# A two-layer encoder trunk on one core: head by quarters of the features, uL, silu and casts earlier in the transitions

## The chip, the cores and the metric

One core of a Trainium2 chip runs the whole program in one launch. The metric is the device time of one execution in microseconds. TensorE does the matmuls, VectorE (DVE in the profile), ScalarE (ACT) and GpSimd (POOL) do the rest, and SyncE (SP) issues the transfers from HBM.

## The reference, cut to what matters

Two layers, each an FFN, a token mixer and an FFN; x is 256 tokens by 1024 features, float32.

```python
for layer in range(DEPTH):
    mod = (silu(c) @ w_ada[layer] + b_ada[layer]).reshape(b, N_SUB, 3, 1, D_MODEL)
    u = standardize(x) * (1 + mod[:, 0, 1]) + mod[:, 0, 0]
    g, up = split(u @ w_ffn_in[layer, 0], 2)                  # 1024 x 5632
    f = (silu(g) * up) @ w_ffn_out[layer, 0]                  # 2816 x 1024
    x = layer_norm(ALPHA * x + 0.5 * (1 + mod[:, 0, 2]) * f, ln_g[layer, 0], ln_b[layer, 0])
    u = standardize(x) * (1 + mod[:, 1, 1]) + mod[:, 1, 0]
    m = hybrid_mixer(u, positions, ...)                       # SSD heads and attention heads
    x = layer_norm(ALPHA * x + (1 + mod[:, 1, 2]) * m, ln_g[layer, 1], ln_b[layer, 1])
    ...                                                       # a second FFN, as the first
```

`mod` is one vector of nine chunks of 1024 for each layer: shift, scale and gate for each of three sublayers.

## The kernel before, in words

Tokens lie in two tiles of 128, t = 0 and 1. Every operand of a large product is kept as a high part (a cast to float32r) and a low part (what the cast left over), and a product is three matmuls: high by high, high by low, low by high. For activations the parts are `uH` and `uL`, for weights `h...` and `l...` (`hg` and `lg` of the gate, `hu` and `lu` of the up half, `ho` and `lo` of the output weights, `hqk` and `lqk` of the mixer's first columns). The high part of a weight is a cast on ACT (`hi`, "h" in the orders), the low part a subtraction on VectorE (`step`, "l" or "a"), 128 x 1024 elements each.

Weights stream in one planned list of 512 KB halves. `issue_loads` keeps nine raw buffers filled; a buffer is free when the subtraction, or the sum of a modulation vector, has read it. The modulation rows are summed against silu(c): on VectorE in the stream, and in the head chunk 0 (shift) on TensorE and chunk 1 (scale) on VectorE (`adh_step`).

The **head** is the first FFN's beginning. It runs through the list `HEAD`, by two halves of the 1024 features: statistics of a tile (n), rstd (r), normalise and turn (x), sums (a), copying them (c), making columns of them (p), modulation of the half (m), weight casts (h, l), the high and low products of columns block b, gate or up i (`U`, `L`), silu and multiplication (e, `evac_a`), turning h (t). This order is strict on TensorE, VectorE and ACT: `in_order(True, pe=True)` makes each engine issue in the order of the program.

Behind it come **blocks** of 256 hidden columns. Block b makes `ob` (48 matmuls of 256 columns for each of two halves j), then the output product of block b-1 (`acc`, 512 columns); silu and a multiplication `hf` turn `ob` into h, which `split` gives parts hH and hL. Here the order within an engine is made by a scheduler from priorities, save for ties set by `order` and `keep`.

Between two sublayers `cross` runs a **transition**: the same residual and norm chain for both tiles (c0 and c1: gate, mean, acc, rstd, squares, rstd2, turn, us, u, m0, l0, m1, and l1 at the end), with the rest of the old sublayer's products (d0 to d3), weight casts (h, l) and the first products of the next sublayer for tile 0 (`P` columns, parts, k range; part 0 is uH by high weights, 1 uL by high weights, 2 uH by low weights) between the steps. The strings FFN_TO_MIX, MIX_TO_FFN and FFN_TO_FFN are that order, and it is strict on all three engines. In such a string "0 m0" makes `um` of tile 0's first half on ACT, "0 l0" subtracts uH from it to give uL on VectorE, and "e" (`evac0`) evacuates the first product bank: an ACT copy before a mixer, silu on ACT and hf on VectorE before an FFN. There are two transitions from FFN to mixer, two from mixer to FFN and one from FFN to FFN.

`setup_mixer` makes the mixers' constants (rotary angles, exponentials) and is called in the blocks of the first FFN.

Of the kernel before, what the change touches and what calls it, by code (L numbers as in the profile page):

```python
# [20 lines left out]
P = 128  # L21
# [21 lines left out]
XAT = 2  # L43
# [5 lines left out]
              "1 acc,P01 02 07,l,1 rstd,0 m0,1 squares,P2 0 07,P2 2 03,P3 0 03,0 l0,P01 1 03,P23 1 03,P3 0 47,1 rstd2,0 m1,"  # L49
              "1 turn,0,P01 1 47,1 us,1 u,l,P2 2 47,P23 1 47,l,l,e,P3 2 07,1,h,h,h").split(",")  # L50
MIX_TO_FFN = ("l,d0,h,h,d1,d2,d3,0 mean,h,0 acc,0 rstd,0 squares,l,0 rstd2,h,0 turn,1 gate,1 gate,0 us,0 u,1 mean,"
              "1 acc,P01 02 07,l,1 rstd,0 m0,1 squares,h,P2 0 07,P2 2 03,P3 0 03,0 l0,P01 1 03,P23 1 03,P3 0 47,1 rstd2,0 m1,"
              "1 turn,0,P01 1 47,1 us,1 u,l,P2 2 47,P23 1 47,l,l,e,P3 2 07,1,h").split(",")
FFN_TO_FFN = ("h,l,d0,0 mean,d1,0 acc,0 rstd,h,h,d2,d3,0 squares,l,0 rstd2,h,l,h,h,0 turn,1 gate,1 gate,0 us,0 u,1 mean,"
              "1 acc,P01 02 07,l,1 rstd,0 m0,1 squares,P2 0 07,P2 2 03,P3 0 03,0 l0,P01 1 03,P23 1 03,P2 2 47,P3 0 47,"
              "1 rstd2,0 m1,1 turn,0,P01 1 47,1 us,1 u,l,l,e,P23 1 47,P3 2 07,1,h").split(",")
# [8 lines left out]
HEAD = ("b,n0,r0,a,n1,x0,a,a,a,c0,r1,x1,a,a,a,p0,a,p1,h,m,h,h,l,l,h,l,h,l,U00,a,U01,a,L00,L01,a,a,c0,U10,a,a,U11,"  # L65
        "a,h,a,p0,L10,p1,L11,+,h,m,k,h,h,h,l,l,U00,l,U01,l,h,l,L00,L01,e00,h,U10,e10,l,h,l,U11,t00,h,l,L10,t10,l,"
        "L11,h,l,e01,t01,h,l,e11,h,l,t11").split(",")

@with_exitstack
def kernel(  # L70
# [124 lines left out]
    def issue_loads(upto):  # L195
        while pos["load"] < min(upto, 2 * len(items)):
            n = pos["load"]
            i, h = divmod(n, 2)
            kind, key, src = items[i]
            if kind == "pair":  # L200
                half = src[h].rearrange("(k p) c -> p k c", p=P)
            else:
                half = src.rearrange("(h k p) c -> h p k c", h=2, p=P)[h]
            shape = {"cols": [4, BC], "pair": [4, BC], "adh": [2, 512]}.get(kind, [1, D])
# [15 lines left out]
    ADA = ("ada", "adh")  # L220

    def hi_step():
# [6 lines left out]
        shape = [D] if kind == "rows" else [4, BC]  # L229
# [11 lines left out]
    def step(n=1):  # L241
        for _ in range(n):
# [6 lines left out]
            if kind in ADA:  # L249
                pos["hi"] = max(pos["hi"], k + 1)  # L250
                {"ada": ada_step, "adh": adh_step}[kind](key, raws.pop(k), h)
# [36 lines left out]
    def setup_cond():  # L288
        crow = tp.tile([KT, P], F32, tag="row8", name="crow", bufs=1)
        nc.sync.dma_start(crow, c_in.rearrange("o (k p) -> (o k) p", p=P))  # L290
        nc.sync.dma_start(xs[:, 0, :], x_in[0, 0:P, :])
# [4 lines left out]
        issue_loads(XAT)  # L296
        nc.sync.dma_start(xs[:, 1, :], x_in[0, P:2 * P, :])
# [44 lines left out]
    half_mods = {}  # L342

    def adh_step(key, raw, k):
        ch, h, q = key
        if ch == 1:
            if q == 0 and k == 0:
                half_mods[ch] = wtile([512], f"adv_{h}")
            acc = half_mods[ch]
            for i in range(2):  # L350
                kt = 4 * q + 2 * k + i
                if kt == 0:
                    V.tensor_scalar(acc, raw[:, i, :], cT[:, 0:1], None, op0=ALU.mult)
                else:
                    V.scalar_tensor_tensor(acc, raw[:, i, :], cT[:, kt:kt + 1], acc, op0=ALU.mult, op1=ALU.add)
            return
        if q == 0 and k == 0:
            half_mods[ch] = mps(f"adh{ch}_{h}")
        pa = half_mods[ch]
        for i in range(2):  # L360
            j = 32 * (2 * k + i)
            PE.matmul(pa[j:j + 32, :], lhsT=cw[:, 4 * q + 2 * k + i, :], rhs=raw[:, i, :],
                      start=(q == 0), stop=(q == 1), tile_position=(0, j))

    def adh_copy(h):
        cpy = wtile([512], f"adc_{h}")
        S.copy(cpy, half_mods[0])
        half_mods[0] = cpy

    def adh_post(ch, h):  # L370
        cpy = half_mods.pop(ch)
        if (0, 0) not in mods:
            mods[0, 0] = sm.tile([P, 2, KT], F32, tag="mod", name="mod0_0", bufs=3)
        pp = mps(f"pm_{ch}_{h}")
        for k in range(4):
            PE.matmul(pp[:, k:k + 1], lhsT=cpy[:, k * P:(k + 1) * P], rhs=ones[:, 0:1] if ch else sel1,
                      start=True, stop=True)
        V.scalar_tensor_tensor(mods[0, 0][:, ch, 4 * h:4 * h + 4], pp[:, 0:4], float(ch),
                               bcol[0][:, ch * KT + 4 * h:ch * KT + 4 * h + 4], op0=ALU.add, op1=ALU.add)
# [260 lines left out]
    class Ffn:  # L640
# [41 lines left out]

        def evac(self, o, name):
            sg = tp.tile([P, BC], F32, tag="sg", name="sg" + name)
            S.activation(sg, o[:, 0:BC], AF.Silu)
            hf = tp.tile([P, BC], F32, tag="hf", name="hf" + name)
            V.tensor_tensor(hf, o[:, BC:2 * BC], sg, op=ALU.mult)
            return hf
# [24 lines left out]
        def plan_head(self):  # L713
            for h in range(2):
                for ch in range(2):
                    for q in range(2):
                        plan("adh", (ch, h, q), w_ada[0, q * 512:(q + 1) * 512, ch * D + h * 512:ch * D + (h + 1) * 512])
                r = slice(h * 512, (h + 1) * 512)
                for b in range(NA):
                    plan("pair", f"{b}_{h}", [self.win[r, c + b * BC:c + (b + 1) * BC] for c in (0, DFF)])  # L720

        def head(self):

            norm, pts, ws = {}, {}, {}

            def form(b, i, low):
                if low == 0 and i == 0:
                    ws[b] = take("pair", f"{b}_{half}")
                for t in range(T):
                    if (t, b) not in self.oa:  # L730
                        self.oa[t, b] = gps(f"oa_{t}{b}") if b == 0 else apt(f"oa_{t}{b}")
                    o = self.oa[t, b][:, i * BC:(i + 1) * BC]
                    w = ws[b][i][low]
                    for n, a in enumerate((uH,) if low else (uH, uL)):
                        for k in range(4):
                            PE.matmul(o, lhsT=a[:, t, 4 * half + k, :], rhs=w[:, k, :],
                                      start=(half == 0 and i == 0 and low == 0 and n == 0 and k == 0),
                                      stop=(half == 1 and i == 1 and low == 1 and k == 3))

            half, got = 0, [0, 0]  # L740
            for fn in HEAD:
# [6 lines left out]
                elif op == "x":  # L748
                    for h in range(2):
                        pts[args[0], h] = turn_norm(0, 0, args[0], *norm[args[0]], h, apt(f"pt_{args[0]}_{h}"))  # L750
# [4 lines left out]
                elif op == "s":  # L755
                    setup_mixer()
                elif op == "c":
                    adh_copy(got[0])
                elif op == "p":
                    adh_post(args[0], got[args[0]])  # L760
                    got[args[0]] += 1
                elif op == "m":
                    advance(modulate(0, 0, {(t, half): pts[t, half] for t in range(T)}))
# [636 lines left out]
```

## Time and profile before

| | |
|---|---|
| three runs | 1075.52, 1075.60, 1075.69 us (median 1075.6) |
| profiled execution | 1074.92 us, span 1073.2 us |
| TensorE busy | 1031.1 us, 96% of the span |
| VectorE busy | 825.4 us, 77% |
| ACT busy | 580.9 us, 54% |
| mean rate of the transfers | 239 GB/s |

The profiled execution's time is its span, from the first instruction to the last, and 1.7 us around it. Times in rows are microseconds from the span's start. A window's PEclk is the clock that TensorE was granted: 1.00 is 2.4 GHz and 0.50 is 1.2 GHz. Ends of matmuls are modelled, so starts are the better measure of pace. An idle time in square brackets is the engine's wait before an instruction, with what ended it.

### The profile page before, as it was taken

What the parts mean: (1) busy time and instruction counts of PE and PEld (TensorE: products, weight loads), DVE (VectorE), ACT (ScalarE), POOL (GpSimd) and SP (SyncE); (2) the same over time, 40 slices, a digit from 0 to 9 for tenths busy, and PEclk for the clock granted to TensorE, in tenths of its full rate; (3) what the DMA queues carried; (4) which work ended last, traced back from release to release, by engine and by line L of the source; (5) the groups of instructions that cost most, each with busy time, mean ns of one, the idle gap of its engine ahead of it and who ended that gap; (6) DMA issues with size and microseconds to landing.
All of it is one profiled execution on the core that took longest, in us unless ns stands there. A gap on an engine that the chain in (4) does not pass through costs nothing.

```text
span 1073.2 us, 19053 instructions
## 1 busy us (share of the span) xinstructions
PE 1031.1 (96%) x7433; PEld 944.3 (88%) x7433; DVE 825.4 (77%) x1284; ACT 580.9 (54%) x1046; POOL 36.1 (3%) x79
## 2 busy tenths in 40 slices
PE   4999999989999999999999999999999999999996
PEld 2899999879897899999989999998899879999995
DVE  5788699688998798768588868847899878756454
ACT  3474434378756755343477433536876578535241
POOL 0000000010000100000010000000000010000000
PEclk9999999999999999999999999999999999999998
DMA  9989799948456389879547979883664628866411
GB/s 341 319 298 370 273 306 407 306 138 254 134 188 225 99 304 341 286 294 361 199 138 249 335 296 377 282 280 107 199 209 150 213 91 302 282 221 216 158 41 39
DMA packets 162559, 258.25 MB, mean 241 GB/s; under 512 B 10807, under 2 KB 125983, under 8 KB 162469
## 3 DMA queue, kind: packets, MB, share of 16 engines
q1 hardware_dynamic: 162468, 257.04, 69.6%
q8 instruction: 58, 0.95, 0.4%
q14 instruction: 33, 0.26, 0.1%
HBM read 255.96 MB, written 1.05 MB: 239 GB/s over the span
## 4 chain that ended last, share of the span: by engine, by line
PE 77%; DVE 10%; ACT 7%; issue 3%; DMA 2%; POOL 1%; SPq 0%; DVEq 0%; POOLq 0%; ACTq 0%
PE ob L108 38%; PE acc L108 18%; PE oa L108 5%; PE ocx L108 2%; PE accx L108 2%; PE ovx L108 2%; DVE xs L108 2%; ACT uH L108 2%; ACT um L108 1%; PE oqkx L108 1%; PE ozx L108 1%; ACT junk L108 1%; DVE acc L108 1%; PE pr L108 1%; DVE lg L108 1%
## 5 line engine op out<-in xcount | busy, mean ns | idle before, releaser
L108 PE MATMUL ob<-uH,hg 128*128 128x256 f32 x576 | 162.6, 282 | 0.0
L108 PE MATMUL ob<-uL,hg 128*128 128x256 f32 x576 | 162.2, 282 | 0.0
L108 PE MATMUL ob<-uH,lg 128*128 128x256 f32 x576 | 161.8, 281 | 0.3 <-DVE lg L108 0.3
L108 PE MATMUL ob<-uH,lu 128*128 128x256 f32 x576 | 162.0, 281 | 0.0
L108 PE MATMUL ob<-uH,hu 128*128 128x256 f32 x576 | 161.9, 281 | 0.0
L108 PE MATMUL ob<-uL,hu 128*128 128x256 f32 x576 | 161.7, 281 | 0.0
L108 PE MATMUL acc<-ho,hH 128*128 128x512 f32 x352 | 137.5, 392 | 1.0 <-ACT ho L108 1.0
L108 PE MATMUL acc<-lo,hH 128*128 128x512 f32 x352 | 137.8, 391 | 0.7 <-DVE lo L108 0.7
L108 PE MATMUL acc<-ho,hL 128*128 128x512 f32 x352 | 137.2, 390 | 0.0
L108 ACT ACTIVATE sgb<-ob 128x256 f32<-128x256 f32 x72 | 27.6, 383 | 202.2 <-PE ob L108 201.8
L108 DVE TENSOR_TENSOR lo<-raw_o,ho 128x1024 fp32r<-128x1024 f32 x88 | 105.6, 1220 | 14.4 <-ACT ho L108 7.2
L108 PEld LDWEIGHTS ob<-uH,hg 128*128 128x128 f32 x576 | 108.3, 188 | 6.2 <-issue 2.5
L108 PEld LDWEIGHTS ob<-uH,lu 128*128 128x128 f32 x576 | 110.1, 191 | 1.2 <-issue 1.2
L108 PEld LDWEIGHTS ob<-uH,lg 128*128 128x128 f32 x576 | 110.2, 191 | 0.6 <-DVE lg L108 0.5
L108 PEld LDWEIGHTS ob<-uL,hg 128*128 128x128 f32 x576 | 108.1, 188 | 2.5
L108 DVE TENSOR_TENSOR lg<-raw_g,hg 128x1024 fp32r<-128x1024 f32 x84 | 101.2, 1221 | 11.2 <-ACT hg L108 5.6
L108 PEld LDWEIGHTS ob<-uH,hu 128*128 128x128 f32 x576 | 108.4, 188 | 0.5 <-issue 0.4
L108 PEld LDWEIGHTS ob<-uL,hu 128*128 128x128 f32 x576 | 108.1, 188 | 0.0
L108 DVE TENSOR_TENSOR lu<-raw_u,hu 128x1024 fp32r<-128x1024 f32 x84 | 100.3, 1219 | 3.4 <-PE ob L108 1.7
L108 ACT CAST hg<-raw_g 128x1024 fp32r<-128x1024 f32 x84 | 86.9, 1056 | 28.1 <-PE acc L108 17.8
L108 DVE TENSOR_TENSOR hfb<-ob,sgb 128x256 f32<-128x256 f32 x72 | 30.3, 420 | 91.2 <-ACT sgb L108 91.0
L108 ACT CAST ho<-raw_o 128x1024 fp32r<-128x1024 f32 x88 | 90.2, 1049 | 12.7 <-PE ob L108 9.0
(535 smaller groups left out, 2307.1 us busy)
## 6 DMA issues: line engine op xcount, KB each, us to landing
raw_o<-in_w_ffn_out_dram SPq DMA_DIRECT2D x88, 512.0 KB, 5.8
raw_g<-in_w_ffn_in_dram SPq DMA_DIRECT2D x84, 512.0 KB, 5.6
raw_u<-in_w_ffn_in_dram SPq DMA_DIRECT2D x84, 512.0 KB, 6.1
raw<-in_w_ffn_in_dram SPq DMA_DIRECT2D x8, 512.0 KB, 8.1
lg<-in_ln_g_dram SPq DMA_DIRECT2D x6, 512.0 KB, 6.0
lb<-in_ln_b_dram SPq DMA_DIRECT2D x6, 512.0 KB
raw_qk0x<-in_w_in_dram SPq DMA_DIRECT2D x4, 512.0 KB, 3.6
raw_qk1x<-in_w_in_dram SPq DMA_DIRECT2D x4, 512.0 KB
```

The source lines that it names most:

```text
L108: ins = emit(*args, **kwargs)
```

## The change

The head goes by four quarters of 256 features. The modulation loads become quarters (`adq`), both chunks are summed on TensorE (`adq_step`, four matmuls side by side for each load), copied and turned to columns in one go. The weights of a quarter come as gate and up halves of 512 columns (two blocks at once), so products have 512 columns. x is turned once and kept as `xT` on SBUF, and `modulate_quarter` makes uH on ACT and um and uL on VectorE from it. The second x tile is loaded before the modulation rows. In the transitions "0 l0" moves ahead of "1 squares", "P3 0 47" joins "P3 0 03", "e" moves ahead of "1 u", and in MIX_TO_FFN an "h" moves from behind "1 squares" ahead of "0 turn". In the last block of the first FFN all casts are issued before the block's products, silu is ordered after them, and the first two casts of the next sublayer (`PRE`) after the split. The constants of `setup_mixer` are tied behind the casts issued before them.

```diff
-FFN_TO_MIX = (... "1 acc,P01 02 07,l,1 rstd,0 m0,1 squares,P2 0 07,P2 2 03,P3 0 03,0 l0,P01 1 03,P23 1 03,P3 0 47,1 rstd2,0 m1,"
-              "1 turn,0,P01 1 47,1 us,1 u,l,P2 2 47,P23 1 47,l,l,e,P3 2 07,1,h,h,h")
+FFN_TO_MIX = (... "1 acc,P01 02 07,l,1 rstd,0 m0,0 l0,1 squares,P2 0 07,P2 2 03,P3 0 07,P01 1 03,P23 1 03,1 rstd2,0 m1,"
+              "1 turn,0,P01 1 47,1 us,e,1 u,l,P2 2 47,P23 1 47,l,l,P3 2 07,1,h,h,h")
-MIX_TO_FFN = (... "0 squares,l,0 rstd2,h,0 turn,1 gate,1 gate,0 us,0 u,1 mean,"
-              "1 acc,P01 02 07,l,1 rstd,0 m0,1 squares,h,P2 0 07,P2 2 03,P3 0 03,0 l0,P01 1 03,P23 1 03,P3 0 47,1 rstd2,0 m1,"
-              "1 turn,0,P01 1 47,1 us,1 u,l,P2 2 47,P23 1 47,l,l,e,P3 2 07,1,h")
+MIX_TO_FFN = (... "0 squares,l,0 rstd2,h,h,0 turn,1 gate,1 gate,0 us,0 u,1 mean,"
+              "1 acc,P01 02 07,l,1 rstd,0 m0,0 l0,1 squares,P2 0 07,P2 2 03,P3 0 07,P01 1 03,P23 1 03,1 rstd2,0 m1,"
+              "1 turn,0,P01 1 47,1 us,e,1 u,l,P2 2 47,P23 1 47,l,l,P3 2 07,1,h")
-FFN_TO_FFN = (... "1 acc,P01 02 07,l,1 rstd,0 m0,1 squares,P2 0 07,P2 2 03,P3 0 03,0 l0,P01 1 03,P23 1 03,P2 2 47,P3 0 47,"
-              "1 rstd2,0 m1,1 turn,0,P01 1 47,1 us,1 u,l,l,e,P23 1 47,P3 2 07,1,h")
+FFN_TO_FFN = (... "1 acc,P01 02 07,l,1 rstd,0 m0,0 l0,1 squares,P2 0 07,P2 2 07,P3 0 07,P01 1 03,P23 1 03,"
+              "1 rstd2,0 m1,1 turn,0,P01 1 47,1 us,e,1 u,l,l,P23 1 47,P3 2 07,1,h")
-HEAD = ("b,n0,r0,a,n1,x0,a,a,a,c0,r1,x1,a,a,a,p0,a,p1,h,m,h,h,l,l,h,l,h,l,U00,a,U01,a,L00,L01,a,a,c0,U10,a,a,U11,"
-        "a,h,a,p0,L10,p1,L11,+,h,m,k,h,h,h,l,l,U00,l,U01,l,h,l,L00,L01,e00,h,U10,e10,l,h,l,U11,t00,h,l,L10,t10,l,"
-        "L11,h,l,e01,t01,h,l,e11,h,l,t11")
+HEAD = ("b,n0,n1,r0,a,a,x0,r1,a,a,c,x1,p,m,h,h,l,l,"
+        "U00,a,a,U010,a,a,c,L00,p,U011,L01,m,h,h,l,l,"
+        "U10,a,a,U110,a,a,c,L10,p,U111,L11,m,h,h,l,l,k,"
+        "U20,a,a,U210,a,a,c,L20,p,U211,L21,m,h,h,l,l,"
+        "U300,U310,L300,L310,e00,U301,U311,e01,L301,L311,h,t00,e10,h,t01,l,e11,l,t10,h,l,t11,h,l")
...
-        nc.sync.dma_start(xs[:, 0, :], x_in[0, 0:P, :])
+        for t in range(T):
+            nc.sync.dma_start(xs[:, t, :], x_in[0, t * P:(t + 1) * P, :])
...
+    def adq_step(key, raw, k):
+        ch, q = key
+        if ch == 0 and k == 0:
+            quarter["sum"] = mps(f"adq_{q}")
+        for i in range(4):
+            PE.matmul(quarter["sum"][32 * i:32 * i + 32, ch * BC:(ch + 1) * BC], lhsT=cw[:, 4 * k + i, :],
+                      rhs=raw[:, i, :], start=(k == 0), stop=(k == 1), tile_position=(0, 32 * i))
+
+    def adq_copy(q):
+        quarter["rows"] = wtile([512], f"adc_{q}")
+        S.copy(quarter["rows"], quarter["sum"])
+
+    def adq_post(q):
...
         for k in range(4):
+            PE.transpose(pp[:, k * P:(k + 1) * P], quarter["rows"][:, k * P:(k + 1) * P], ident)
+        col = sm.tile([P, 4], F32, tag="mc", name=f"mc_{q}", bufs=1)
+        V.tensor_reduce(col, pp.rearrange("p (c j r) -> p c j r", c=4, j=4)[:, :, :, 0], axis=AX.X, op=ALU.add)
+        for w in range(2):
+            V.scalar_tensor_tensor(mods[0, 0][:, w, 2 * q:2 * q + 2], col[:, 2 * w:2 * w + 2], float(w),
+                                   bcol[0][:, w * KT + 2 * q:w * KT + 2 * q + 2], op0=ALU.add, op1=ALU.add)
...
+            for q in range(4):
+                r = slice(q * BC, (q + 1) * BC)
                 for ch in range(2):
+                    plan("adq", (ch, q), w_ada[0, :, ch * D + q * BC:ch * D + (q + 1) * BC])
+                plan("pair", q, [self.win[r, c:c + NA * BC] for c in (0, DFF)])
...
+            def turn(t):
+                for h in range(2):
+                    pt = turn_norm(0, 0, t, *norm[t], h, apt(f"pt_{t}_{h}"))
+                    S.copy(xT[h][:, :, t, :], pt.rearrange("p (k c) -> p k c", k=4))
+
+            def modulate_quarter(q):
+                md = mods[0, 0]
+                um = tp.tile([P, 2, T, P], F32, tag="u", name=f"um_{q}", bufs=3)
+                for k in range(2):
+                    kk = 2 * q + k
+                    src = xT[kk // 4][:, kk % 4]
+                    sh, sc = [md[:, w, kk:kk + 1] for w in range(2)]
+                    S.activation(uH[:, :, kk, :], src, AF.Identity, bias=sh, scale=sc)
+                    V.tensor_scalar(um[:, k], src, sc, sh, op0=ALU.mult, op1=ALU.add)
+                for k in range(2):
+                    kk = 2 * q + k
+                    V.tensor_tensor(uL[:, :, kk, :], um[:, k], f(uH[:, :, kk, :]), op=ALU.subtract)
+
+            def form(q, i, tt, low):
+                w = tiles["pair", q][i][low]
+                for t in tt:
...
                     for n, a in enumerate((uH,) if low else (uH, uL)):
+                        for k in range(2):
+                            PE.matmul(banks[t, i], lhsT=a[:, t, 2 * q + k, :], rhs=w[:, k, :],
+                                      start=(q == 0 and low == 0 and n == 0 and k == 0),
+                                      stop=(q == 3 and low == 1 and k == 1))
...
-                    target = done["rows", f"o{self.nm}_{b}"] + (PRE if nxt else 0)
+                    target = done["rows", f"o{self.nm}_{b}"] + (PRE if nxt and self.nm != "00" else 0)
...
-                    step((target - pos["lo"] + 1 - j) // (2 - j))
+                    step(target - pos["lo"] if j or (self.nm == "00" and b == NB - 1) else (target - pos["lo"] + 1) // 2)
+                    cast = stream["a"] if j == 0 else cast
...
                     hf = self.evac(o, f"b{self.nm}_{b}{j}")
+                    ends = self.nm == "00" and b == NB - 1 and j == 1
+                    if ends:
+                        order(self.silu, cast)
+                        in_order(True)
                     hH, hL = self.hts[b]
                     split(hf, hH[:, j, :], hL[:, j, :])
+                    if ends:
+                        step(PRE)
...
-        V.tensor_copy(posf, posi)
+        order(V.tensor_copy(posf, posi), stream["v"])
...
-        S.activation(nega, nega, AF.Exp)
+        order(S.activation(nega, nega, AF.Exp), stream["a"])
```

## Rows read from the trace of the kernel before

**Rows 1.** The page, part 1: busy time, share of the span, instructions.

```profile
PE 1031.1 (96%) x7433; PEld 944.3 (88%) x7433; DVE 825.4 (77%) x1284; ACT 580.9 (54%) x1046; POOL 36.1 (3%) x79
```

**Rows 2.** Windows: length, busy PE, PEld, DVE, ACT, POOL, PEclk, DMA share, GB/s.

```profile
0.00:23.00 23.00, 9.94 (x51) 5.59 (x51) 12.34 (x29) 6.35 (x12) 2.63 (x13) 1.00 0.92 330
23.00:29.80 6.80, 4.36 (x19) 3.68 (x20) 5.85 (x10) 5.48 (x9) 0.00 (x0) 0.50 1.01 369
...
90.00:206.00 116.00, 115.63 (x860) 107.43 (x859) 95.88 (x105) 50.31 (x73) 0.95 (x1) 1.00 0.93 331
```

**Rows 3.** Waits of TensorE over the span: total us, times, longest.

```profile
PE oa L108 <- DVE uL L108: 4.2, 6, 1.4
...
PE oqkx L108 <- DVE uL L108: 3.6, 4, 1.6
...
PE oa L108 <- DVE hfa L108: 1.1, 3, 0.5
PE acc L108 <- ACT ho L108: 1.0, 1, 1.0
...
PE acc L108 <- DVE lo L108: 0.7, 2, 0.5
```

**Rows 4.** The chain that ended last, head and first block: start, us, what.

```profile
25.50 3.79 PE oa L108 x16
30.56 2.08 PE oa L108 x16
...
69.88 2.73 PE acc L108 x12
72.61 5.65 PE ob L108 x48
```

**Rows 5.** Timeline of the head, ACT and PE: start, us, instruction, [idle before].

```profile
17.45 0.58 ACT L108 COPY adc<-adh 128x512 f32<-128x512 f32 x1 [3.39 <-PE adh L108]
19.83 1.05 ACT L108 CAST h<-raw 128x1024 fp32r<-128x1024 f32 x1 [1.79 <-DMA raw<-in_w_ffn_in_dram]
...
32.56 1.05 PE L108 MATMUL adh<-raw_(0, 1, 0)_1_228,cw 128*32 128x512 f32 x4
```

**Rows 6.** Timeline of the first transition from mixer to FFN: DVE, PE, ACT.

```profile
363.54 0.68 DVE L108 TENSOR_TENSOR uL<-um,uH 128x512 fp32r<-128x512 f32 x1
366.74 1.05 PE L108 MATMUL ptp<-ident,xn 128*128 128x128 f32 x8
367.38 2.90 ACT L108 ACTIVATE uH<-ptp,mod 128x128 fp32r<-128x128 f32 x8 [0.30 <-PE ptp L108]
368.86 2.36 DVE L108 TENSOR_TENSOR lu<-raw_u,hu 128x1024 fp32r<-128x1024 f32 x2
370.30 1.28 ACT L108 ACT_TABLE_LOAD   x1
371.59 0.38 ACT L108 ACTIVATE sga<-oa 128x256 f32<-128x256 f32 x1
372.01 0.42 DVE L108 TENSOR_TENSOR hfa<-oa,sga 128x256 f32<-128x256 f32 x1 [0.79 <-ACT sga L108]
372.49 0.73 PE L108 MATMUL oa<-hg,uH 128*128 128x256 f32 x4 [0.48 <-DVE hfa L108]
```

**Rows 7.** Timeline of DVE at the head's end.

```profile
57.28 1.22 DVE L108 TENSOR_TENSOR lu<-raw_u,hu 128x1024 fp32r<-128x1024 f32 x1 [0.45 <-ACT hu L108]
```

**Rows 8.** Timeline at the first FFN's end, ACT and DVE.

```profile
212.87 1.99 ACT L108 CAST ho<-raw_o 128x1024 fp32r<-128x1024 f32 x2
...
220.11 0.69 DVE L108 TENSOR_TENSOR acc<-acc,gate 128x512 f32<-128x512 f32 x1
```

**Rows 9.** Timeline of PE in the transition from FFN to FFN.

```profile
563.98 1.04 PE L108 MATMUL ptp<-ident,xn 128*128 128x128 f32 x8
...
568.30 0.97 PE L108 MATMUL oa<-hg,uH 128*128 128x256 f32 x6 [0.46 <-DVE hfa L108]
```

More of the change, by code (lines that the diff above doesn't have):

```diff
@@ L42 @@
 NRAW = 9
-XAT = 2
 AHEAD = 9
@@ L228, in hi_step @@
         issue_loads(n + 1)
-        shape = [D] if kind == "rows" else [4, BC]
+        shape = {"rows": [D], "pair": [2, 512]}.get(kind, [4, BC])
         ht, lt = [wtile(shape, f"{e}{key}_{h}", F32R) for e in "hl"]
@@ L339, in ada_step @@
             late.append(lambda: ada_post(l, s, w, adas.pop((l, ch))))
[L342 to L372, printed above, removed]
+    quarter = {}
+    def adq_step(key, raw, k):
[5 more added lines that the diff above has]
+                      rhs=raw[:, i, :], start=(k == 0), stop=(k == 1), tile_position=(0, 32 * i))
@@ L681, in htile, with gated @@
                            hp.tile([P, 2, SEQ], F32R, tag="hL", name=f"hL{self.nm}_{b}"))
-        def evac(self, o, name):
[L684 to L688, printed above, removed]
+        def gated(self, g, u, name):
+            sg = tp.tile([P, BC], F32, tag="sg", name="sg" + name)
+            self.silu = S.activation(sg, g, AF.Silu)
+            hf = tp.tile([P, BC], F32, tag="hf", name="hf" + name)
+            V.tensor_tensor(hf, u, sg, op=ALU.mult)
+            return hf
+        def evac(self, o, name):
+            return self.gated(o[:, 0:BC], o[:, BC:2 * BC], name)
         def mm_a(self, t, b):
@@ L722, in head @@
-        def head(self):
[L724 to L733, printed above, removed]
-                    for n, a in enumerate((uH,) if low else (uH, uL)):
[L735 to L740, printed above, removed]
+                    plan("adq", (ch, q), w_ada[0, :, ch * D + q * BC:ch * D + (q + 1) * BC])
@@ L748, in head @@
                 elif op == "x":
-                    for h in range(2):
-                        pts[args[0], h] = turn_norm(0, 0, args[0], *norm[args[0]], h, apt(f"pt_{args[0]}_{h}"))
+                    turn(*args)
                 elif op == "b":
@@ L754, in head @@
                     load_mixer()
[L755 to L763, printed above, removed]
-                elif op == "+":
-                    half = 1
+                elif op in "cpm":
+                    {"c": adq_copy, "p": adq_post, "m": modulate_quarter}[op](q[op])
+                    q[op] += 1
                 elif op == "h":
@@ L770, in head @@
                 elif op in "UL":
-                    form(*args, int(op == "L"))
+                    form(args[0], args[1], args[2:] or range(T), int(op == "L"))
                 elif op == "e":
-                    self.evac_a(*args)
+                    evac(*args)
                 elif op == "t":
                     self.turn_a(*args)
+            for q in range(4):
+                del tiles["pair", q]
             in_order(False)
```

47 lines of the change are left out of this document (22 added, 25 removed).

## The prediction

> **What bounds the kernel now.** I read the page first, then the windows, then what TensorE waited for, then the chain that ended last, and last the order of instructions at the places which the diff touches. TensorE is busy for 1031.1 us of the span [rows 1], and over the nine streamed blocks of the first FFN it has practically no gap (115.63 of 116 us in the last window of [rows 2]). Time can be won only where TensorE stands, and lost only where a new stall appears on it. It stands in three kinds of places. In the head (the first 58 us) it is busy 9.94 of the first 23 us [rows 2]. At the transitions the waits for uL add up to 4.2 and 3.6 us and those for hfa to 1.1 us; at the end of the first FFN the waits for ho and lo are 1.0 and 0.7 us [rows 3]. Everything else is products at a fixed pace: 2.73 us for 12 of 512 columns and 5.65 us for 48 of 256 [rows 4], so 0.227 and 0.118 us each.
>
> **The head.** It removes the sixteen VectorE steps on chunk 1 of the first modulation and two late rounds of sums; it adds more work on TensorE for both chunks, four sums copied and turned, and xT copies. The products are the same in number of columns: 24 of 512 columns per quarter, 5.45 us. TensorE now sums both chunks. A load's two matmuls of 512 columns, side by side in the array, take 1.05 us [rows 5]. A load of the change has four side by side, each half as wide, which no row shows; between 0.53 us (half the row) and 2.1 (twice it, if four do not run together) I take 0.53, since only the width counts if they do.
>
> The loads are as many bytes as before. The eleventh 512 KB load was there at 19.83 [rows 5]; at the 369 GB/s of the next window [rows 2] a load takes 1.42 us, so the 24th (last modulation load) lands about 38.3 and the 26th (last weights) about 41.1. One quarter's chain on the other engines is: copy of the sums 0.58 [rows 5]; low products of the gate half 0.91 beside it; four transposes 0.5; a reduction of 16 elements, which no row shows, 0.2 (nothing below, the 0.42 of a 256-wide VectorE operation above, [rows 6]); two small additions 0.25 together; two modulating ACT operations of 256 columns, 0.38 each by the silu of that shape [rows 6]; the cast of the gate's weights 1.05 [rows 5], which is queued behind them on ACT. With handovers that is 3.75 us. Before it stand 8 products (1.82), two loads' sums (1.07), 4 products (0.91) and two sums (1.07). A quarter thus takes 8.6 us; its loads take 6 x 1.42 = 8.5, so both are nearly equal and the last loads are not what it waits for. The second x tile is issued ahead of the modulation loads and sets the first of them back by one load; the small loads of the mixers' constants move behind the second quarter's weights. Both are hidden by the lead of the last loads, 41.1 against 44.3 where their cast starts; without it they would cost one load, 1.42.
>
> The first products stood at 25.50 [rows 4]. In the change both x tiles and the first four sums must be through, then four copies, and the casts behind them. I estimate 19.5 us, since the pair lands four loads (5.7 us) earlier and its cast no longer waits for VectorE sums; 18 and 22 bound it. The last quarter then begins its products at B = 19.5 + 3 x 8.6 = 45.3.
>
> Behind B the order written out by hand decides. The products end at B+5.7. VectorE must do, in order: two low casts of the quarter, hf, hf, hL, hf, hL, and only then the first low cast of block 2. The hL wait for hH copies, and ACT runs a 1.05 us cast between the two. That low cast (1.22 us, [rows 7]) ends at B+9.8; the other three follow with hf or hL between them at B+11.3, B+12.8 and B+14.3. Each releases 12 of the 48 products of block 2 (1.41 us), so these end at B+15.8 = 61.1. With the 24 products of the first output rows (5.45) the state is reached at 66.6 that the old kernel reaches at 69.88 [rows 4]. Gain 3.3 us. Bounds: 0 if the first quarter starts at 22 and the sums cost a little more; 9 if block 2 does not wait for low casts (B+5.7+5.65+5.45 is 62.1, and 1.5 earlier with an early start). Later blocks keep the gain: VectorE is busy 95.88 of 116 us there [rows 2], and is freed of nothing that block 2 needs.
>
> **Mixer constants.** Same operations, issued in block 4 instead of the head's end, with four table loads of 1.28 us each [rows 6] on ACT. ACT is busy 50.31 of 116 us there [rows 2]; cost 0, and up to 1.3 if one delays a silu that feeds the next block.
>
> **End of the first FFN.** The last two ho casts ran at 212.87, behind the last silu [rows 8], and TensorE waited 1.0 + 0.7 us for them and lo [rows 3]. Now they precede it. VectorE can start its gate multiplications, at 220.11 before [rows 8], earlier by the two low casts (2 x 1.22) at most, because two casts of the next sublayer still stand between. The transition's chain is ruled by those. I take 2.0 us; 0.8 if the bias sum on ACT now falls between, 2.6 at most.
>
> **The transitions.** l0 (uL, 0.68 us, [rows 6]) now stands ahead of the two xs operations of tile 1. The uL wait on TensorE goes. But tile 1's chain (xs, squares, rstd, xn, transposes) is later by 0.4 to 1.1 us, because l0 itself waits for the um operations of ACT. TensorE has no other work left then, since P3 0 47 was drawn ahead: what stood before P01 1 03 now stands before the turn. In the two FFN-to-mixer transitions, where the moved step is one ACT copy and VectorE has no part in it, I count a loss of 1.0 us together (0 to 1.4).
>
> The silu is the larger thing. Its hf multiplication is in VectorE's strict queue, now *ahead* of the low casts ("l") that P2 2 47 and P3 2 07 need; before, those casts filled the time (lu from 368.86 for 2.36, hfa at 372.01, [rows 6]). Worked through from the start of tile 1's transposes (366.74): 0.64 to the first uH on ACT, half of the eight uH 1.45, the table load 1.28, silu 0.38, hf 0.42 with handovers 0.1, so hf is done at +4.3; three low casts 3.5; the last four products 0.5: tile 1's own products start at +8.3. Before it was 372.49 - 366.74 = 5.75 [rows 6], and about 0.2 more went to one of the six uL waits of [rows 3] directly after. The loss is 2.3 and with the later transposes (0.5) 2.8 us, twice (mixer to FFN): 5.6. In the FFN-to-FFN transition no table load is needed, silu waits for the products P01 1 47 (+2.1), hf is done at +2.95, two low casts 2.35, four products 0.5: +5.8, against 568.30 - 563.98 = 4.3 before [rows 9], with 0.2 of the same waits gone: loss 1.3. Nothing on TensorE covers these stalls, because its queue there is strict too. Bounds for the three together: 3 (low casts come partly before) and 8. The cast that MIX_TO_FFN draws ahead of tile 0's transposes runs while ACT waits for these; cost 0, 1.05 without that.
>
> A rule of the Trainium skill bears on the silu. The row shows a table load of 1.28 us, 0.02 after the operation before it ended and 0.01 before the silu [rows 6]. The skill ("ScalarE: Activation LUTs", "What ACT_TABLE_LOAD costs") counts about 1.38 us of draining on top, 2.66 in all. By it each mixer-to-FFN transition would lose 1.4 us more than by the row; the row shows no such gap, and I go by the row.
>
> **Sum.** Head -3.3, end of the first FFN -2.0, FFN-to-mixer +1.0, mixer-to-FFN +5.6, FFN-to-FFN +1.3: +2.6 us. The profiled execution took 1074.92 us, so it would become 1077.5; the median of the runs is 0.7 above that execution, so I forecast 1078.2.
>
> **Rivals.**
> *The silu costs nothing (faster).* If hf does not hold back the low casts, the 6.9 us go and 2.6 becomes -4.3: 1071.3. For it: in three old transitions TensorE did wait for hfa [rows 3]. Against: the low casts have the same queue. It decides once hf ends before the low cast of P2 2 47 could have started. Chance 0.12.
> *The head gives all its 9 us (faster).* 2.6 - 5.7: 1072.5. For it: the last loads land 3 us before they are needed. Against: the low casts behind hf and hL. It decides if the first low cast of block 2 ends by B+6. Chance 0.10.
> *The clock falls in the head (slower).* From 23.0 to 29.8 the granted clock was 0.50, the 1.2 GHz level, after TensorE had stood for want of modulation sums [rows 2]; 16 products took 3.79 us there and 2.08 at 2.4 GHz [rows 4]. A stretch of the same length inside the quarters costs half of 6.8 us, 3.4: 1081.6. For it: TensorE stands about 2 us before its first products and 0.6 per quarter. Against: it stands less than before. Chance 0.17, with the lower end of the head's gain in it. The skill's rule ("TensorE: Matmul & The Clock Gate", "Part 1: The HAM clock gate") is that half rate is the default and idling brings it back; the trace agrees that it fell behind a gap.
> *The change undoes itself.* Head and first FFN gain as much as the transitions lose, within 2 us: 1075.6, chance 0.12. For it: both sums are over 5 us and independent.
> *The drain of the skill's table rule.* Twice 1.4 more: 1081.0; against it are the 0.02 us of the row; chance 0.02.
>
> **How the numbers follow.** The forecast has 0.47, in 1076.2 to 1080.2. A measurement here tells some 0.2% (2.15 us) from no change, so slower begins at 1077.75: about two thirds of the forecast's chance lies above. Slower 0.31 + 0.17 + 0.02 = 0.50; faster 0.12 + 0.10 = 0.22; same 0.16 + 0.12 = 0.28. The range 1072.0 to 1081.8 holds the forecast, the full head and most of the clock case, and leaves out the free silu and the upper half of the clock case, about 0.2.
>
> **What would show it.** Head: the last quarter's products start near 45, and TensorE then waits some 3 us for lg of block 2. End of the first FFN: no waits for ho and lo. Mixer to FFN: a wait of TensorE for lg and lu (together 3 us) after the transposes of tile 1, with VectorE idle before hfa for 2.5 us; waits for uL become waits for xn. FFN to FFN: the same with 1.3 us. Wrong it is if VectorE's low casts still come before hfa, if the quarters take under 8 us, or if the wait for lg in the head is missing.

## The result and the profile after

The changed kernel takes 1084.87 us (median of 4 runs, 1082.12 to 1085.78); the kernel before takes 1075.56 beside it (4 runs). The ratio is 1.0087, 95% interval 1.0065 to 1.0109: 9.3 us slower. The forecast was 2.6 us slower, in a range that ended at 1081.8. The direction was right, the size was not. The profiled execution took 1084.60 us, its span is 1082.9.

The page's part 1, the windows and TensorE's waits of the changed kernel answer to [rows 1 to 3]:

```profile
PE 1033.3 (95%) x7417; PEld 940.5 (87%) x7417; DVE 814.8 (75%) x1280; ACT 584.3 (54%) x1049; POOL 38.4 (4%) x79
```

```profile
18.00:20.66 2.66, 0.01 (x2) 0.00 (x1) 1.92 (x8) 2.27 (x5) 0.00 (x0) 1.00 1.08 393
20.66:23.30 2.64, 2.64 (x6) 2.17 (x7) 2.34 (x2) 0.89 (x1) 0.00 (x0) 0.50 1.06 399
...
90.00:206.00 116.00, 113.92 (x842) 105.16 (x841) 97.90 (x131) 58.05 (x82) 0.95 (x1) 1.00 0.92 323
...
246.00:252.40 6.40, 5.72 (x28) 5.43 (x27) 4.52 (x10) 5.84 (x17) 0.00 (x0) 0.50 0.72 209
```

```profile
PE ptp L109 <- DVE xn L109: 10.6, 6, 1.9
PE oa L109 <- ACT h L109: 5.0, 4, 2.6
PE oa L109 <- DVE hfa L109: 4.4, 2, 2.2
...
PE acc L109 <- ACT hH L109: 2.1, 2, 1.1
...
PE pr L109 <- DVE ada L109: 0.9, 1, 0.9
...
PE oa L109 <- DVE uL L109: 0.6, 1, 0.6
```

TensorE's busy time grew by 2.2 us and the span by 9.7, so most of the loss is TensorE standing. The change did what its lines say. The waits for uL are nearly gone (4.2 and 3.6 us in [rows 3], 0.6 here), and those for ho and lo are gone. In their place came 10.6 us for xn, 4.4 for hfa and 2.1 for hH. Leaving out the end of the span, where both kernels drop to it, the changed kernel ran TensorE for 10.2 us at its lower level of 1.2 GHz (20.67 to 24.09 and 245.95 to 252.78), the kernel before for 6.8 (23.01 to 29.84, [rows 2]). At half speed that is about 1.7 us more, an estimate that takes TensorE as busy all the while.

Where the time went is read from one instruction that both kernels have in every transition, the first of tile 0's transposes (ptp):

| Start, us | before | after | after minus before | gained since the line above |
|---|---|---|---|---|
| first FFN to mixer | 229.90 | 233.22 | +3.3 | +3.3 |
| mixer to FFN | 356.16 | 361.31 | +5.2 | +1.8 |
| FFN to FFN | 552.70 | 560.38 | +7.7 | +2.5 |
| second FFN to mixer | 746.86 | 754.14 | +7.3 | -0.4 |
| second mixer to FFN | 871.47 | 879.77 | +8.3 | +1.0 |
| end of the span | 1073.2 | 1082.9 | +9.7 | +1.4 |

Each step of the last column holds the transition named in the line above and the sublayer behind it. Head and first FFN, forecast to win 5.3 us, lost 3.3. The transitions lost 6.3, near the 7.9 forecast, but that is in part luck: FFN to mixer lost 2.8 where 1.0 was forecast, mixer to FFN 3.9 where it was 5.6, and FFN to FFN nothing where it was 1.3. The first step of +1.8 contains the second stretch at 1.2 GHz.

**The head.** The chain that ended last, answering to [rows 4]; columns are start, us, instruction. It shows the start of the first quarter's products, one quarter whole, then B, the start of the last quarter's products, and the state that the prediction aimed at.

```profile
20.66 3.68 PE oa L109 x8
...
31.62 2.11 PE oa L109 x8
33.73 1.00 PE adq L109 x16
34.73 1.12 PE oa L109 x4
35.85 1.00 PE adq L109 x16
36.85 1.14 PE oa L109 x4
37.98 0.45 PE pm L109 x4
38.46 0.18 DVE mc L109
38.66 0.24 DVE mod L109 x2
38.99 1.09 ACT uH L109 x2
40.09 0.94 ACT h L109
41.07 2.11 PE oa L109 x8
...
50.49 5.87 PE oa L109 x24
...
71.41 2.74 PE acc L109 x12
```

From 20.66 to 50.49 only TensorE, VectorE and ACT stand in this chain, no transfer. A quarter takes 9.45 us, and in its last 2.65 TensorE has work for 1.84 and then waits 0.81 for h. The state "first half of block 2 and 24 output products" is reached at 71.41, 1.5 later than the 69.88 of [rows 4].

**The end of the first FFN**, ACT's timeline, answering to [rows 8]:

```profile
215.16 0.39 ACT L109 ACTIVATE sgb<-ob 128x256 f32<-128x256 f32 x1 [3.55 <-PE ob L109]
217.32 1.06 ACT L109 ACTIVATE lb<-lb 128x1024 f32<-128x1024 f32 x1 [1.78 <-DMA lb<-in_ln_b_dram]
...
218.38 0.39 ACT L109 CAST hH<-hfb 128x256 fp32r<-128x256 f32 x1
```

The bias sum, which runs over lb, stands in ACT's queue ahead of the last hidden copy. Its load had not landed, so ACT stood 1.78 us. The copy hH, the casts of the next sublayer and TensorE's last products (0.96 us) waited behind it.

**The first transition from mixer to FFN**, timelines of VectorE and ACT, answering to [rows 6]:

```profile
376.49 0.42 DVE L109 TENSOR_TENSOR hfa<-oa,sga 128x256 f32<-128x256 f32 x1 [2.99 <-ACT sga L109]
376.83 1.22 DVE L109 TENSOR_TENSOR lg<-raw_g,hg 128x1024 fp32r<-128x1024 f32 x1
...
374.78 1.28 ACT L109 ACT_TABLE_LOAD   x1
376.07 0.38 ACT L109 ACTIVATE sga<-oa 128x256 f32<-128x256 f32 x1
...
392.54 1.05 ACT L109 CAST hg<-raw_g 128x1024 fp32r<-128x1024 f32 x1 [2.71 <-DMA raw_g<-in_w_ffn_in_dram]
393.50 0.64 ACT L109 CAST hH<-ph 128x256 fp32r<-128x256 f32 x2
```

VectorE stands 2.99 us in front of hfa with three low casts queued behind it, as forecast. Its wait shows on TensorE under the name of hfa (2.2 us), not of lg or lu. Later two copies hH stand behind a cast whose weights had not landed, and TensorE waits 1.1 us for them.

### The profile page after: what moved, and what is told of

Same layout as the page of the kernel before. It is cut to its first block, busy times and chain, and to the rows that moved or that the text cites. A ratio compares the mean times of both kernels' runs of the same rounds, so it can differ in the third digit from the quotient of the medians.

```text
span 1082.9 us, 19036 instructions
## 1 busy us (share of the span) xinstructions
PE 1033.3 (95%) x7417; PEld 940.5 (87%) x7417; DVE 814.8 (75%) x1280; ACT 584.3 (54%) x1049; POOL 38.4 (4%) x79
## 3 DMA queue, kind: packets, MB, share of 16 engines
HBM read 255.96 MB, written 1.05 MB: 237 GB/s over the span
## 4 chain that ended last, share of the span: by engine, by line
PE 75%; DVE 10%; ACT 8%; DMA 3%; issue 3%; POOL 1%; SPq 0%; DVEq 0%; POOLq 0%; ACTq 0%
PE ob L109 36%; PE acc L109 16%; PE oa L109 4%; PE oqkx L109 3%; PE ocx L109 3%; ACT junk L109 2%; PE ovx L109 2%; PE accx L109 2%; DVE xs L109 2%; DMA lb<-in_ln_b_dram 1%; ACT uH L109 1%; ACT um L109 1%; PE ozx L109 1%; PE pr L109 1%; PE adq L109 1%
```

## The experiments

All ratios below are to the kernel before on the same chip; one thousandth is 1.08 us. A difference of two of them is uncertain by 1.3 to 1.8 us, and by some 2.6 where the change's own ratio of 4 runs is one of them.

**Parts of the transitions.** Three kernels undo a part of them in the changed kernel. e1 puts the silu back (the same edit in all three strings, shown for one):

```diff
-1 turn,0,P01 1 47,1 us,e,1 u,l,P2 2 47,P23 1 47,l,l,P3 2 07
+1 turn,0,P01 1 47,1 us,1 u,l,P2 2 47,P23 1 47,l,l,e,P3 2 07
```

> The changed kernel with the silu of the first tile put back to its old place in all three transitions; the early l0 and the new order of products stay. Theory A (from the two traces): the silu's new place is a help. In the old kernel TensorE went on 5.75 us after tile 1's transposes began, in the changed one 4.38 us, so the early silu gives 1.37 us per mixer-to-FFN transition, and the loss comes from l0 and the products drawn ahead. Then this is slower than the change by 2 x 1.4 = 2.7 us: 1087.6. Theory B (the prediction): the silu's multiplication holds the low casts back for 2.8, 2.8 and 1.3 us. Then this is faster than the change by 6.9 us: 1078.0.

Measured: 1.0049 (1.0037 to 1.0061), 1080.74 us. The silu's new place costs about 4.1 us when l0 is early too. Theory A, which read the shorter stretch behind the transposes as a help, is refuted.

e2 puts l0 and the products back and leaves the silu up:

```diff
-1 rstd,0 m0,0 l0,1 squares,P2 0 07,P2 2 03,P3 0 07,P01 1 03,P23 1 03,1 rstd2
+1 rstd,0 m0,1 squares,P2 0 07,P2 2 03,P3 0 03,0 l0,P01 1 03,P23 1 03,P3 0 47,1 rstd2
```

> The changed kernel with the old transitions in which only the silu of the first tile is moved up: l0 and the products of part 3 stand where they stood before. Theory A: the transitions' losses as the traces show them (1.8 and 1.0 in FFN to mixer, 2.9 and 1.4 in mixer to FFN, 0.2 in FFN to FFN, 7.3 in all) go, and TensorE's waits for xn of 1.4 to 1.9 us with them; the waits for uL come back. 1077.6, or up to 1 us less since the early silu helps. Theory B: l0 and the products cost 1.0 us and the silu's 6.9 stay: 1083.9.

Measured: 1.0042 (1.0030 to 1.0054), 1079.83 us, 4.8 us better than the change. This lies between the two theories: beside the early silu, l0 and the products cost more than forecast.

e3 takes all three old strings:

> The changed kernel with all three orders of the transitions as before, so new head, constants and end of the first FFN alone. Theory A: the 7.3 us that the transitions lose in the trace are all theirs: 1077.6, which is 2 us slower than before, because the head and the end of the first FFN give nothing (head +1.5, later blocks +1.6, end -0.5). Theory B (the prediction): head -3.3 and end -2.0 are won, so it is faster than before by 5: 1070.3.

Measured: 1.0028 (1.0017 to 1.0038), 1077.95 us. The transitions cost 6.3 us of the 9.3 (1.0087 less 1.0028). Without them the kernel is still slower than before, so the head and the end of the first FFN win nothing. Against e3, l0 and the products alone (e1) cost 2.3 us, and the silu alone (e2) 1.5, which is not clear of the uncertainty. The two do not add up to 6.3; why they cost more together is not shown.

**The silu taken apart.** On the kernel with the old transitions and the bias sum moved (e5, below), e12 moves the silu and its multiplication up in the transitions into an FFN. e11 moves the silu alone and leaves the multiplication behind the low casts (E):

```diff
 e12
-1 us,1 u,l,P2 2 47,P23 1 47,l,l,e,P3 2 07
+1 us,e,1 u,l,P2 2 47,P23 1 47,l,l,P3 2 07
 e11
+1 us,e,1 u,l,P2 2 47,P23 1 47,l,l,E,P3 2 07
         def evac0(self):
-            self.evac_a(0, 0)
+            S.activation(self.sg0, self.oa[0, 0][:, 0:BC], AF.Silu)
+        def multiply0(self):
+            V.tensor_tensor(hf, self.oa[0, 0][:, BC:2 * BC], self.sg0, op=ALU.mult)
```

> The same kernel with silu and multiplication moved up in the two transitions into an FFN and nothing else. Theory B (the prediction): 2 x 2.8 + 1.3 = 6.9 us slower than 1.0005: 1.0069. Theory C (from the traces of the kernels with and without it: 2.5 in the first mixer to FFN, where the copy hH then stood behind a cast that waited for its load, 0.6 in the second, 0.2 in FFN to FFN): about 2.2 to 3.3 us slower, 1.0025 to 1.0035.

> As the kernel with new head, new end, bias sum moved and old transitions (1.0005), but with the silu of the first tile moved up in the two transitions into an FFN, and its multiplication on VectorE left at the old place behind the low casts. Theory B (the prediction: the multiplication in front of the low casts is what costs): nothing is lost, 1.0005 or a little better. Theory C: the table load and the silu between the two halves of uH are what costs; then it is as slow as with the multiplication moved too, 1.0025.

Measured: e12 1.0049 (1.0037 to 1.0061), e11 1.0007 (0.9998 to 1.0017), e5 1.0005. The silu and its table load cost nothing that can be told where they now stand. The multiplication ahead of the low casts costs 4.7 us against e5. VectorE in the first mixer-to-FFN transition, e11 and then e12:

```profile
366.55 1.22 DVE L109 TENSOR_TENSOR lg<-raw_g,hg 128x1024 fp32r<-128x1024 f32 x1
367.69 2.36 DVE L109 TENSOR_TENSOR lu<-raw_u,hu 128x1024 fp32r<-128x1024 f32 x2
369.96 0.42 DVE L109 TENSOR_TENSOR hfa<-oa,sga 128x256 f32<-128x256 f32 x1
```

```profile
371.15 0.42 DVE L109 TENSOR_TENSOR hfa<-oa,sga 128x256 f32<-128x256 f32 x1 [2.80 <-ACT sga L109]
371.49 1.21 DVE L109 TENSOR_TENSOR lg<-raw_g,hg 128x1024 fp32r<-128x1024 f32 x1
372.62 2.35 DVE L109 TENSOR_TENSOR lu<-raw_u,hu 128x1024 fp32r<-128x1024 f32 x2
```

With the multiplication behind, the three casts fill the time in which ACT gets to the silu, and hfa waits for nothing. With it ahead, VectorE stands 2.80 us. TensorE does not wait for lg then: in the trace eight products of hg by uH, which are tile 1's, come ahead of the first low ones, and they wait for hfa, which reads the bank of tile 0's first products:

```profile
371.63 0.58 PE L109 MATMUL oa<-hg,uH 128*128 128x256 f32 x1 [2.02 <-DVE hfa L109]
```

e2 has the same stall, yet there the silu cost 1.5 us and not 4.7. Windows over the stall and what follows, e2 first, then e12:

```profile
369.59:371.62 2.03, 0.01 (x2) 0.01 (x1) 0.48 (x2) 2.02 (x4) 0.00 (x0) 1.00 0.00 0
371.62:375.00 3.38, 3.38 (x27) 3.33 (x28) 3.38 (x4) 3.38 (x11) 0.00 (x0) 1.00 0.37 99
```

```profile
369.60:371.60 2.00, 0.01 (x1) 0.00 (x0) 0.45 (x2) 1.99 (x4) 0.00 (x0) 1.00 0.00 0
371.60:375.00 3.40, 3.37 (x15) 3.37 (x16) 3.40 (x4) 3.40 (x11) 0.00 (x0) 0.50 0.33 90
```

In 3.4 us TensorE did 27 products in the one profile and 15 in the other, where the granted clock was 0.50 behind the stall.

Every run comes with its mean granted clock, so this can be followed over all runs. It averages 0.9966 in e5 and 0.9934 in e12 (0.992 to 0.997), but 0.9957 in e3 and 0.9966 in e2 (0.995 to 0.998). A mean lower by 0.0032 over 1080 us is 3.4 us, an estimate that takes TensorE as busy all the while and is uncertain by about 1 us. Among runs of one kernel, a mean lower by 0.001 goes with some 0.65 us (all kernels pooled), which would make 2.1 us of it. So the clock accounts for some 2 to 3.4 of e12's 4.7 us and for none of e2's 1.5. The stall itself is worth 1.3 to 2.7 us, and about half or more of the multiplication's price in e12 is that TensorE slows down behind it. By the same estimate the clock takes up to 2.9 of the 6.3 us of the transitions (0.9930 in the change, 0.9957 in e3), and could be all of e1's 2.3 (0.9932). Why e2 keeps its clock behind the same stall is open.

**The end of the first FFN.** e4 moves the bias sum in the changed kernel, e5 does the same with the old transitions, and e7 is the old kernel with this end alone:

```diff
-        S.activation(lb, lb, AF.Identity, accum_out=slb)
+        if (l, s) != (0, 0):
+            bias_sum(lb, slb)
...
                     if ends:
                         step(PRE)
+                        bias_sum(*rows[1:])
```

> The changed kernel with one step moved: the sum over the normalization's bias at the end of the first FFN (ACT, on lb) is issued behind the last hidden copy and the two casts instead of before it. Theory A: in the changed kernel ACT stood 1.78 us for the landing of lb, and the copy hH, on which TensorE waited 0.96 us, and the casts of the next sublayer stood behind it; without it the copy runs 2.3 us earlier, the gate multiplications start 2.1 us earlier, and the time is 1082.6. Rival: the gate multiplications are held by the low casts, which wait for something else (a load), so nothing changes: 1084.9.

> New head, constants and end of the first FFN, the old transitions, and the bias sum of the first FFN's end behind the casts. Theory A: the bias sum in front of the last hidden copy cost the whole gain of the end of the first FFN; without it 1.6 to 2.0 us come on top of the kernel with the old transitions (1.0028 of before, 3.0 us slower): 1.0009, about 1 us slower than before. Rival: the end of the first FFN gave its 2 us already and the rest is lost elsewhere: 1.0028 as without the edit.

> The old kernel with one part of the change alone, the end of the first FFN, and the bias sum behind the casts; old head, old constants, old transitions. Theory A: the waits for ho and lo (0.99, 0.53, 0.17 us) go and the gates start 2 us earlier: 0.998 to 0.9985 of before, 1.6 to 2.0 us faster; the new head with the constants then costs the difference to the kernel with the new head, 2.6 us. Rival (the prediction's head): the new head is worth 3.3 us, so this kernel is slower than the one with the new head by 3 us: 1.003 if that one is at 1.0.

Measured: e4 1.0052 (1.0040 to 1.0064), 3.8 us better than the change; e5 1.0005 (0.9996 to 1.0014), 2.5 us better than e3; e7 0.9978 (0.9969 to 0.9986), 2.4 us faster than before. ACT in e4:

```profile
212.80 0.39 ACT L109 ACTIVATE sgb<-ob 128x256 f32<-128x256 f32 x1 [3.54 <-PE ob L109]
213.68 0.41 ACT L109 CAST hH<-hfb 128x256 fp32r<-128x256 f32 x1 [0.49 <-DVE hfb L109]
...
215.89 1.06 ACT L109 ACTIVATE lb<-lb 128x1024 f32<-128x1024 f32 x1
```

hH now runs 0.49 us after the silu, once hfb is there, where it had needed 2.83. The idea of this part was right and worth 2.4 us; one instruction in ACT's queue took it all. The new head with the constants costs the difference between e5 and e7, 2.9 us. The clock does not explain this: its mean is 0.9966 in e5 and 0.9939 in e7, so the new head loses less by it than the old one.

**The constants.** e8 is e5 without the four ties that hold the mixers' constants in block 4:

```diff
-        order(S.activation(nega, nega, AF.Exp), stream["a"])
+        S.activation(nega, nega, AF.Exp)
```

> As the kernel with the old transitions and the bias sum moved, but the four first operations of the mixers' constants are no longer tied behind the casts of block 4, so they run as early as in the old kernel. Theory A: in block 4 they held VectorE so that the last modulation sums were late and TensorE waited 0.86 us for them, with 0.2 us later: 0.9 to 1.0 us less, 1.0000 of before. Rival: at the old place they cost as much in the head's end: no difference, 1.0009.

Measured: 1.0003 (0.9993 to 1.0014): no difference that can be told. Windows over the streamed blocks, e5 and then e8:

```profile
90.00:206.00 116.00, 113.91 (x851) 105.44 (x850) 98.73 (x131) 56.37 (x79) 0.95 (x1) 1.00 0.92 322
```

```profile
90.00:206.00 116.00, 115.61 (x856) 106.87 (x856) 93.34 (x105) 49.56 (x73) 0.95 (x1) 1.00 0.91 325
```

TensorE stands 2.1 us there in e5 (0.86 for the modulation sums, 0.2 behind them, 0.50 for hg and 0.52 for lg near 200) and 0.4 in e8, as in the kernel before [rows 2]. But at the head's end of e8 the wait for hfa is 2.2 us instead of 0.9, and in its profile the clock fell there too. The rival holds: in the new kernel the constants cost about the same at either place.

**The head.** e6 is e5 with one cast per quarter drawn ahead of the modulation; e10 is e6 with VectorE's order behind the last quarter changed:

```diff
 e6, in each quarter
-a,a,c,L20,p,U211,L21,m,h,h,l,l
+a,a,c,h,L20,p,U211,L21,m,h,l,l
 e10
-L301,L311,h,t00,e10,h,t01,l,e11,l,t10,h,l,t11,h,l
+L301,L311,h,l,e10,e11,t00,t01,h,l,h,l,t10,t11,h,l
```

> As the kernel with the old transitions and the bias sum moved, and in each quarter of the head the first cast of the weights is issued behind the copy of the sums, ahead of the modulating operations. Theory A: a quarter takes 9.45 us because ACT does the modulation (1.09) and then the cast (1.05) while TensorE stands 0.75 to 0.81; with the cast ahead that wait goes in three quarters and 0.8 to 1.0 us of the 2.65 before the first products: 3.2 us less, 0.998 of before, about 2.2 us faster than before. Rival: the quarter waits for its loads (this is what the prediction thought nearly equal), and the cast drawn ahead stands in ACT's queue until the load is there: no gain, 1.0009.

> As the kernel with the cast drawn ahead in the head (0.9972), and behind the last quarter the first low cast of block 2 and the four multiplications hf stand ahead of the transposed copies and their hL. Theory A: VectorE's strict queue held the low cast behind hL, which waited for hH, for which TensorE's waits of 0.88, 0.49 and 0.81 us stand in the trace; about 1.5 of these 2.2 us go: 0.9958. Rival: the waits only move to the next low casts, which the copies now push back: 0.9972.

Measured: e6 0.9972 (0.9960 to 0.9984), 3.5 us better than e5; e10 0.9954 (0.9942 to 0.9966), 1070.0 us, another 1.9 better, just clear of the uncertainty. ACT in one quarter of e6:

```profile
33.37 0.59 ACT L109 COPY adc<-adq 128x512 f32<-128x512 f32 x1 [4.33 <-PE adq L109]
33.85 1.05 ACT L109 CAST h<-raw 128x1024 fp32r<-128x1024 f32 x1
35.44 1.09 ACT L109 ACTIVATE uH<-xT,mod 128x256 fp32r<-128x256 f32 x2 [0.54 <-DVE mod L109]
```

The cast starts as soon as the copy ends and waits for no transfer, and the next copy stands 8.40 us later (41.77). The head was bound by the order on ACT, not by its loads. With that order mended the loads are near: in e6's last quarter a landing (41.30 to 45.25) stands in the chain that ended last. e10, which is new head, end with the bias sum moved, constants in block 4 and old transitions, beats both kernels, by 0.46% the one before.

**The granted clock.** e9 is the changed kernel with eight transposes of a constant in the stall ahead of tile 1's transposes:

```diff
+        if t == 1 and h == 0 and (l, s) != (0, 0):
+            for k in range(8):
+                PE.transpose(pt[:, 0:P], ident, ident)
```

> The changed kernel as it is, with eight transposes of a constant, about 1.05 us, issued on TensorE ahead of tile 1's transposes in the five transitions, where it stood 1.4 to 1.9 us for xn; their output is overwritten by the real ones. Theory A: the stalls of the early l0 (1.7 to 1.9 us before tile 1's transposes, 0.7 to 2.2 behind them) bring the granted clock to 0.50 for some 4 to 7 us in one transition or another (245.9 to 252.6 in the changed kernel, 886 to 891 with the silu back, 366 to 373.7 and 759.7 to 762.6 with the bias sum moved; none in the two kernels with l0 at its old place). With the stall filled it stays at 1.00 there, and 2 us come back: 1.0068 of before. Rival: the falls have nothing to do with these stalls: 1.0087 as the change.

Measured: 1.0102 (1.0087 to 1.0116), 1085.57 us: not faster. The stalls for xn shrank to about 0.9 us in the mixer-to-FFN transitions, and behind these its profile has no stretch at 0.50; behind the stall for hfa, which was left as it was, there is one, and another (233.84 to 237.25) behind tile 0's stall for xn, which was left too. Windows of e9, the stall for hfa and what follows it:

```profile
371.40:373.60 2.20, 0.03 (x1) 0.03 (x1) 0.51 (x2) 2.19 (x4) 0.00 (x0) 1.00 0.00 0
373.80:377.40 3.60, 3.60 (x19) 3.60 (x19) 3.60 (x4) 3.60 (x11) 0.00 (x0) 0.53 0.47 135
```

A filler at one stall does not give back what the falls cost: the mean granted clock is 0.9937 over its four runs and 0.9930 over the change's, which does not tell them apart.

## Why the prediction failed

Sum against measurement, in us, each measured value a difference of two ratios times 1075.6:

| Term | forecast | measured | from |
|---|---|---|---|
| Head, with the constants | -3.3 | +2.9 | e5 less e7 |
| End of the first FFN | -2.0 | +0.1 | -2.4 (e7) and +2.5 (e3 less e5) |
| The three transitions | +7.9 | +6.3 | change less e3 |
| Sum | +2.6 | +9.3 | |

**The head is the step that failed.** Its first half, "the last quarter then begins its products at B = 45.3", was 5.2 us early in the profile of the change. Its second half, 21.3 us from B to the state, came out (71.41 - 50.49 = 20.9), though not by the parts named: the wait for lg of block 2, forecast at some 3 us, is 0.8, and 1.4 more go to hfa (0.9) and a silu (0.5). The 5.2 us are three terms. The first products started at 20.66, not 19.5. They ran at 0.50 of the clock, 3.68 us where the later quarters took 2.11, which is 1.6. And three quarters took 9.4, not 8.6, which is 2.5. In a quarter, the sixteen products of the chain took 4.37 us (2.11, 1.12 and 1.14), 0.27 each, where the rate of [rows 4] gave 0.227 and 3.6; the two modulating ACT operations took 1.09, not 0.76; the sums and the rest came out 0.2 shorter. The argument that loads and chain were "nearly equal" was beside the point: no load stands in the chain from the first products to B.

Of the three terms the quarters stand in every profile of this head, the fall of the clock in four of ten. In the six without it the first products start at 19.8 to 20.5, B is 48.1 to 48.8 and the state is reached at 69.0 to 69.8. In e5, from the chain that ended last:

```profile
48.45 5.88 PE oa L109 x24
...
69.38 2.74 PE acc L109 x12
```

So without a fall the head wins up to 0.9 us against the 69.88 of [rows 4], not 3.3, and most of what is missing is the 2.5 of the quarters. The rest of the loss lies behind the head, where the prediction says "Later blocks keep the gain" and gives the constants 0 to 1.3. From 90 to 206 TensorE stands 1.7 us more than before (113.92 us busy against the 115.63 of [rows 2]), the same in e5 and not in e8, so it goes with the constants in block 4 (0.50 and 0.52 of it, near 200, may be missing in e8 only because it runs later). In e5's profile the two make 1.2 of the 2.9 us; the other 1.7 are not placed, and are hardly more than the uncertainty of that difference.

**The end of the first FFN.** The gain was sized well (2.0, 2.4 measured). What fell was its condition. The bias sum was named as a risk worth 1.2 us ("0.8 if the bias sum on ACT now falls between"), a price near the sum's own 1.06 us and without a wait for its load. The old kernel ran the sum at 215.72 behind three casts, and ACT waited for nothing there; the change brought the casts out of its way, and the sum to the head of the queue before its load was there.

**The silu.** Theory B of the experiments is the prediction's, and it held: it is the multiplication in front of the low casts that costs. It was sized 5.9 us (2.3 twice and 1.3; the other 1.0 of the 6.9 is the later transposes, which l0 brings). 4.7 were measured with the silu moved in the transitions into an FFN, 1.5 to 4.1 in the other pairs. The agreement with 4.7 is in part luck: up to 3.4 of it is the clock, which the prediction put at nothing in the transitions. Two details were wrong. TensorE's wait has hfa's name, because products of tile 1 stand in front of the low ones. And FFN to FFN, forecast at 1.3, loses nothing that shows: no wait for hfa stands there.

**l0 and the products drawn ahead** cost 2.3 us alone (e1), near the 2.0 of the prediction (1.0 for FFN to mixer and 0.5 for each mixer to FFN), but that may be the clock again, and beside the silu they cost 4.8 (the change less e2). The uL waits became xn waits, as forecast, but with 1.4 to 1.9 us each they are longer than the ones removed (1.0 to 1.6).

**The rivals.** "The clock falls in the head" happened in the profiled execution, with 1.6 us and not 3.4, and a second fall stood where none was forecast, in the first transition. "The head gives all its 9 us" and "the silu costs nothing" did not happen. The Trainium skill ("ScalarE: Activation LUTs", "What ACT_TABLE_LOAD costs") adds a drain of about 1.38 us to a table load. Here the table load of 1.28 us at 374.78 is followed by the silu at 376.07, and e11, with the same table load ahead of the second half of uH, lost nothing: no drain shows.

## What to carry over

In an order written out by hand, price an instruction that moves ahead not by its own duration but by what it waits for, and list what stands behind it in that queue: a 0.42 us multiplication held three casts for 2.8 us, and a 1.06 us sum held a copy for a load. A stall of TensorE can cost more than its length, where the clock falls behind it. Conversely, look in each pipeline stage for an operation that is ready early and stands behind one that is not: one cast per quarter drawn ahead was worth 3.5 us. A stage whose loads and compute seem equal should be summed along the handovers of its chain, with every operation at the duration of its own shape.

## What the runs showed of the hardware

A stall of TensorE sometimes brings its clock down, and the same stall sometimes does not. The stall of 2.65 us or a hundredth more in front of the head's first products stands in ten profiles with the same head. In four (the change, e3, e8, e12) the granted clock was 0.50 behind it, in six (e1, e2, e4, e5, e9, e11) it was 1.00, as in this window of e5:

```profile
17.49:20.15 2.66, 0.00 (x0) 0.00 (x1) 1.92 (x8) 2.33 (x5) 0.00 (x0) 1.00 1.09 391
20.15:22.30 2.15, 2.15 (x12) 1.53 (x16) 2.15 (x2) 0.90 (x1) 0.00 (x0) 1.00 1.05 405
```

The same holds for the stalls of 2.0 us for hfa in e2 and e12, shown above. The fall costs 1.6 us in the head. The Trainium skill ("TensorE: Matmul & The Clock Gate", "Part 1: The HAM clock gate") says that the number of slow products differs from run to run of the same kernel; these profiles agree, though they are of kernels that differ behind the head.

Four matmuls side by side in the array, 32 columns of it each, with 256 columns to stream, take 0.50 us a load (the x16 of two loads at 33.73 in the chain take 1.00), where the two matmuls of 512 columns of a load took 1.05 in [rows 5]. That is twice as many columns in a given time, so the four run together at least in part, as the prediction assumed with its 0.53.
